# Block sums of a seven-product projection: added by DVE, or by accumulating transfers into the loaded block

## The chip, the cores and the metric

The kernel runs on one core of a Trainium2 chip. Its engines are TensorE (PE, with weight loads shown as PEld), VectorE (DVE), ScalarE (ACT), GpSimd (POOL) and SyncE (SP), and 16 DMA engines move data between the chip's main memory and the on-chip SBUF. The metric is the device time of one execution in microseconds. The weights are laid out by the host before the launch; that is not in the time.

## The reference, cut to what matters

Two groups of 512 tokens, each with 1024 features, pass through two layers with the same weights, and a last norm:

```python
for i in range(DEPTH):                       # 2: attention, then retention
    h = rms_norm(x, norm_g[i], NORM_EPS)
    ...
        x = x + diff_attention(h, da_w_in[j], ..., da_w_out[j], lambda_init)
    ...
        x = x + bidir_retention(h, ret_w_in[j], ..., ret_w_out[j])
return rms_norm(x, final_norm_g, NORM_EPS)
```

Both mixers begin with one wide projection, `proj = h @ w_in`, that yields queries, keys, values and a gate. It has 8192 columns in the first layer and 6144 in the second, and it is the projection that the change touches:

```python
proj = h @ w_in
q, k, v, gate = jnp.split(proj, [...], axis=-1)
```

After it, queries and keys are rotated by position, the mixer runs, its output is normed, multiplied by `silu(gate)` and multiplied by `w_out`.

## The kernel before

**Precision.** Every matmul operand is split in two float32r parts, high (`hi_of`, line 383, a cast on ACT) and low (`lo_of`, line 386, a subtraction on DVE), and a product is made of three matmuls: high by high, high by low, low by high (`PASSES`).

**Projection.** The two groups are multiplied by the same weights together. The 1024 input features are cut in two halves (index k) and the output columns of a unit in two halves (index i), so a unit is a product of 2 x 2 blocks for two token groups. It is computed with seven block products instead of eight, after Strassen and Winograd, named P1 to P7. On the side of the activations the sums of blocks are made once per layer (`make_b`). On the side of the weights each unit makes its own: `Unit.prep` at lines 525 to 558. P1, P2 and P4 take a loaded block. P5 takes x(1,0) + x(1,1), P6 takes that less x(0,0), P3 takes x(0,1) less that, P7 takes x(0,0) - x(1,0). These four sums are the calls of `combine` (line 529), DVE instructions of line 532 that write a buffer of the ring `st`. Then the block is split into a place of the ring `ws`, which has 7 places (`WS_BUFS`).

A unit is "pair" (256 columns; a block is 512 rows by 128 columns, 256 KB; a product is 12 matmuls of 512 tokens; one place of `ws`) or "wide" (512 columns of values; a block is 512 KB; a product is 48 matmuls of 256 columns; two places of `ws`). There are 24 pair and 4 wide units in the first layer, 16 and 4 in the second. The pair units are rotated queries and keys (`rot_done`) and gates (`gate_done`); the wide ones are values (`v_done`).

**Loads.** `take` (line 505) loads 512 rows by 256 columns, 512 KB, into one of 4 places of the ring `raw`, four pieces of 1 KB per partition. In a pair unit one load holds x(0,k) and x(1,k) side by side, and `half_view` or `parity_view` picks the columns of one half, which in the first layer are runs of 64 and in the second every other column. The same ring takes the output weights (`out_weights`, line 803) in the mixers' stages. The ring `st` has 3 places and also holds the decay tables of the retention layer (line 1137).

**After the product.** The seven products of a unit accumulate in PSUM banks named x, z and y (`BANK_OF`). ACT copies a bank (line 602) or DVE adds a bank to a copy (line 610); column half i = 0 is finished first, i = 1 later, and the `done` functions (lines 651 to 695) rotate, gate or split the finished half and store it.

**Order.** Nothing is issued directly. Every step is given to a planner (`Plan`) with its engine and an assumed cost, what it reads and what it writes. `Plan.arrange` runs a simulation: each engine takes, of the steps that are ready, the one with the earliest due time; PE may look 24 products ahead; loads are held until 15 us before they are due. Places of a ring are taken in turn. The order found is then issued, and each engine and each queue runs its own part strictly in that order. All transfers but four small ones are issued by SP; POOL makes only the small powers of the norms (lines 739, 740, 849, 851, 935, 936).

The stages are: norm and transposition of x, projections of layer one, attention with the output projection filled in between, projections of layer two, retention with its output projection, last norm.

Of the kernel before, what the change touches and what calls it, by code (L numbers as in the profile page):

```python
# [15 lines left out]
P = 128  # L16
S = 512
# [223 lines left out]
def trunk_kernel(  # L241
    ctx: ExitStack,
    tc: tile.TileContext,
    x_prompt, x_sample, norm_g, da_w_in, lq1, lk1, lq2, lk2, da_subln_g, da_w_out,
    ret_w_in, decay_fwd, decay_bwd, ret_subln_g, ret_w_out, final_norm_g,
# [136 lines left out]
    def hi_of(n, dst, src, r, w):  # L382
        act(n, lambda: nc.scalar.copy(dst(), src()), r, w)  # L383

    def lo_of(n, dst, src, hi, r, w):
        dve(n, lambda: nc.vector.tensor_tensor(dst(), src(), hi().bitcast(F32), op=ALU.subtract), r, w)  # L386
# [106 lines left out]
    class Unit:  # L493
        def __init__(self, w, c0, kind, done, view=None):


            self.w, self.c0, self.kind, self.done = w, c0, kind, done
            self.view = view or (lambda r, i: r[:, :, i * P:(i + 1) * P])
# [4 lines left out]
            self.banks = {}  # L503

        def take(self, i, k):

            if (i, k) not in self.x:
                c0 = self.c0 + (256 * i if self.wide else 0)
                r = slot(self.early + k, [P, 4, 256], F32) if self.early is not None else raw_t([P, 4, 256])
                src = self.w[k * S:(k + 1) * S, c0:c0 + 256].rearrange("(k p) c -> p k c", p=P)  # L510
                dma(lambda: r.t, lambda: src, [], [r], 512)
                if self.wide:
                    self.x[i, k] = ((lambda: r.t), r)
                else:
                    for n in range(2):
                        self.x[n, k] = ((lambda n=n: self.view(r.t, n)), r)
            return self.x[i, k]

        def like(self, t):

            if self.wide or len(self.x[0, 0][0]().shape) == 3:
                return t
            return t.rearrange("p k (j i) -> p k j i", j=2)

        def prep(self, op):
# [3 lines left out]
            def combine(a, b, fn):  # L529
                t = st_t([P, 4, n])  # L530
                out = ((lambda: self.like(t.t)), t)
                dve(4 * n, lambda: nc.vector.tensor_tensor(out[0](), a[0](), b[0](), op=fn), [a[1], b[1]], [t])
                return out
# [20 lines left out]
            hi_of(4 * n, lambda: self.like(hi[0]()), src[0], [src[1]], [hi[1]])  # L554
            lo_of(4 * n, lambda: self.like(lo[0]()), src[0], lambda: self.like(hi[0]()), [src[1], hi[1]], [lo[1]])
# [73 lines left out]
    def rot_done(dst, tab, scaled):  # L629
# [21 lines left out]
        def done(i, g, tiles, s, psum):  # L651
# [20 lines left out]
    def gate_done(dst, gc):  # L672

        def done(i, g, tiles, s, psum):
# [4 lines left out]
            dve(S, lambda: nc.vector.scalar_tensor_tensor(out.t, th.t, 1.0, x.t, op0=ALU.add, op1=ALU.mult),  # L679
# [6 lines left out]
    def v_done(dst):  # L686

        def done(i, g, tiles, s, psum):
            for u, x in enumerate(tiles):
                o = os_t()  # L690
                hi_of(S, lambda o=o: o[:, 0, :], lambda x=x: x.t, [x], [(o, 0)])
                lo_of(S, lambda o=o: o[:, 1, :], lambda x=x: x.t, lambda o=o: o[:, 0, :], [x, (o, 0)], [(o, 1)])
# [175 lines left out]
    w1, wo1, w2, wo2 = da_w_in[0], da_w_out[0], ret_w_in[0], ret_w_out[0]  # L868

    def half_view(r, i):  # L870
        return r.rearrange("p k (j two i) -> p k j two i", j=2, two=2)[:, :, :, i, :]

    def parity_view(r, i):
        return r.rearrange("p k (j i two) -> p k j i two", j=2, two=2)[:, :, :, :, i]
# [11 lines left out]
    def units1(tab):  # L886
        ropes = [Unit(w1, which * DI + h * 256, "pair",
                      rot_done({g: qk_d[0, which, h, g] for g in range(NG)}, tab, which == 0), half_view)
                 for h in range(NH) for which in range(2)]
        gates = [Unit(w1, 3 * DI + h * 256, "pair", gate_done({g: g_d[0, h, g] for g in range(NG)}, 16))  # L890
                 for h in range(NH)]
        wides = [Unit(w1, 2 * DI + h * 256, "wide",
# [4 lines left out]
    def units2(tab2):  # L897
        ropes = [Unit(w2, which * D + h * P, "pair",
                      rot_done({g: qk_d[1, which, h, g] for g in range(NG)}, tab2, which == 1), parity_view)
                 for h in range(0, NH, 2) for which in range(2)]  # L900
        gates = [Unit(w2, 2 * D + DI + h * 256, "pair", gate_done({g: g_d[1, h, g] for g in range(NG)}, 18))
                 for h in range(NH)]
        wides = [Unit(w2, 2 * D + h * 256, "wide",
# [339 lines left out]

def _tables():
# [40 lines left out]
```

## Time and profile before

| | us |
|---|---|
| median of 3 runs | 1864.89 |
| runs | 1857.8 to 1865.54 |
| span of the profiled execution, first to last instruction | 1856.5 |
| start, up to the steady projections | 72 |
| projections of layer one | 556 |
| hand-over and attention | 399 |
| hand-over to layer two | 50 |
| projections of layer two | 433 |
| retention, with its hand-over | 324 |
| last norm | 23 |

The stages are cut by eye from the trace's chain of waits. In the rows of the profile a line such as L386 is a line of the kernel; names left of the arrow are written, right of it are read, with buffer numbers left out; "b" and "arena" hold the activations' operands, "pj", "sc", "o" and "tp" are PSUM banks. A busy PE is not a PE at its peak, since the ends of matmuls are modelled; so the pace is read from the starts of products. Idle time before an instruction is followed by what released it.

### The profile page before, as it was taken

How to read it: one execution, taken by the hardware profiler on the slowest of the kernel's cores; microseconds unless marked ns; L12 is line 12 of the kernel's file. 1: busy time of each engine (PE TensorE's matmuls, PEld its weight loads, DVE VectorE, ACT ScalarE, POOL GpSimd, SP SyncE). 2: the span in 40 equal slices, each digit the busy share in tenths (PEclk: the TensorE clock that was granted, in tenths of full speed). 3: DMA queues.
4: the chain of work that ended last, by engine and by line, in shares of the span. 5: the costliest groups of instructions: out<-in, count | busy, mean ns of one | idle time of the engine just before them, and what ended most of it. 6: DMA issues, size and time to landing. Idle time of an engine off the chain costs nothing.

```text
span 1856.5 us, 27778 instructions
## 1 busy us (share of the span) xinstructions
PE 1823.4 (98%) x10337; PEld 1578.6 (85%) x10337; DVE 1450.6 (78%) x2423; ACT 926.7 (50%) x1897; POOL 152.8 (8%) x372
## 2 busy tenths in 40 slices
PE   6999999999999999999999999999999999999998
PEld 5888988988988878888888888989898988888886
DVE  7979688688688588888888896777777767766777
ACT  6734444343344465555555874435353454444444
POOL 3000000000000011111111300000000001111112
PEclk9999999999999999999999999999999999999999
DMA  4335544545545774444453433553545487434542
GB/s 161 119 119 182 182 136 153 177 124 181 160 126 173 266 272 179 182 170 153 153 183 125 159 97 103 168 170 130 174 143 165 142 313 268 169 146 168 195 145 91
DMA packets 149696, 307.31 MB, mean 166 GB/s; under 512 B 11940, under 2 KB 71992, under 8 KB 149560
## 3 DMA queue, kind: packets, MB, share of 16 engines
q1 hardware_dynamic: 149376, 305.45, 48.6%
q8 instruction: 81, 1.33, 0.3%
q14 instruction: 55, 0.45, 0.1%
q10 hardware_dynamic: 184, 0.08, 0.0%
HBM read 196.43 MB, written 109.05 MB: 165 GB/s over the span
## 4 chain that ended last, share of the span: by engine, by line
PE 91%; DVE 4%; ACT 2%; issue 1%; DMA 1%; POOL 1%; POOLq 0%; DVEq 0%; ACTq 0%
PE pj L573 22%; PE pj L824 18%; PE sc L573 11%; PE pj L580 9%; PE o L573 5%; PE o L1059 5%; PE o L1178 5%; PE sc L580 5%; PE sc L1007 5%; PE o L580 2%; PE sc L1160 2%; PE o L755 1%; PE tp L1043 1%; DVE ws L386 1%; DMA raw<-in_da_w_out_dram 1%
## 5 line engine op out<-in xcount | busy, mean ns | idle before, releaser
L824 PE MATMUL pj<-ws,arena 128*128 128x512 f32 x1536 | 399.5, 397 | 0.0
L824 PEld LDWEIGHTS pj<-ws,arena 128*128 128x128 f32 x1536 | 278.9, 188 | 54.1
L573 PE MATMUL pj<-b,ws 128*128 128x512 f32 x1200 | 293.6, 391 | 0.6 <-DVE e L610 0.6
L573 PEld LDWEIGHTS pj<-b,ws 128*128 128x128 f32 x1200 | 224.7, 188 | 49.6 <-issue 1.0
L829 DVE TENSOR_TENSOR b<-pj,b 128x512 f32<-128x512 f32 x256 | 176.1, 688 | 108.1 <-PE pj L824 107.7
L573 PE MATMUL sc<-arena,ws 128*128 128x512 f32 x960 | 232.3, 392 | 1.9 <-DVE arena L441 1.9
L386 DVE TENSOR_TENSOR ws<-st,ws 128x512 fp32r<-128x512 f32 (+1 forms) x192 | 148.1, 776 | 92.7 <-ACT ws L383 58.4
L573 PEld LDWEIGHTS sc<-arena,ws 128*128 128x128 f32 x960 | 180.1, 188 | 41.4 <-DVE arena L441 2.1
L386 DVE TENSOR_TENSOR ws<-raw,ws 128x512 fp32r<-128x512 f32 (+1 forms) x172 | 147.2, 861 | 83.5 <-ACT ws L383 72.4
L383 ACT CAST ws<-st 128x512 fp32r<-128x512 f32 (+1 forms) x192 | 131.9, 693 | 100.1 <-PE pj L573 35.8
L573 PE MATMUL pj<-arena,ws 128*128 128x512 f32 x720 | 177.5, 392 | 0.2 <-DVE arena L386 0.2
L383 ACT CAST ws<-raw 128x512 fp32r<-128x512 f32 (+1 forms) x172 | 130.8, 766 | 75.6 <-PE o L573 45.4
L739 POOL TENSOR_SCALAR css<-css 128x1 f32<-128x1 f32 x128 | 33.7, 263 | 1631.6 <-ACT o L737 918.3
L573 PEld LDWEIGHTS pj<-arena,ws 128*128 128x128 f32 x720 | 134.6, 188 | 29.3 <-DVE arena L386 0.5
L602 ACT COPY c<-pj 128x512 f32<-128x512 f32 x112 | 65.2, 583 | 128.5 <-PE pj L573 78.6
L573 PE MATMUL o<-arena,ws 128*128 128x512 f32 x480 | 116.0, 392 | 3.0 <-DVE e L441 3.0
L580 PE MATMUL pj<-ws,b 128*128 128x256 f32 x960 | 116.8, 276 | 0.0
L580 PEld LDWEIGHTS pj<-ws,b 128*128 128x128 f32 x960 | 113.2, 188 | 0.7
L1023 ACT ACTIVATE b<-sc,nm 128x512 f32<-128x512 f32 x128 | 88.0, 687 | 50.6 <-DVE nm L1015 50.5
L573 PEld LDWEIGHTS o<-arena,ws 128*128 128x128 f32 x480 | 89.4, 188 | 22.3 <-ACT ws L383 3.0
L1059 PE MATMUL o<-arena 128*128 128x256 f32 x768 | 106.8, 289 | 0.0
L1007 PE MATMUL sc<-arena 128*128 128x512 f32 x384 | 100.6, 398 | 4.0 <-ACT b L1023 4.0
(162 smaller groups left out, 2896.8 us busy)
## 6 DMA issues: line engine op xcount, KB each, us to landing
qk<-os SPq DMA_DIRECT2D x192, 256.0 KB, 3.9
arena<-qk SPq DMA_DIRECT2D x80, 512.0 KB, 4.8
raw<-in_da_w_in_dram SPq DMA_DIRECT2D x64, 512.0 KB, 5.1
v<-os SPq DMA_DIRECT2D x64, 512.0 KB, 4.2
arena<-v SPq DMA_DIRECT2D x64, 512.0 KB, 4.4
raw<-in_ret_w_in_dram SPq DMA_DIRECT2D x48, 512.0 KB, 4.2
os<-g SPq DMA_DIRECT2D x32, 512.0 KB, 7.5
g<-e SPq DMA_DIRECT2D x48, 256.0 KB, 4.4
```

Source lines behind the costliest of these rows:

```text
L383: act(n, lambda: nc.scalar.copy(dst(), src()), r, w)
L386: dve(n, lambda: nc.vector.tensor_tensor(dst(), src(), hi().bitcast(F32), op=ALU.subtract), r, w)
L573: nc.tensor.matmul(ps.t, a[u][0]()[:, k, :], bt[k][:, v, :], start=(opens and k == 0 and i == 0), stop=(k == 3 and i == 2), skip_group_che ...
L580: nc.tensor.matmul(ps[:, (t % 2) * 256:(t % 2) * 256 + 256], bt[k][:, v, t * P:(t + 1) * P], a[u][0]()[:, k, :], start=(opens and t % 2 == ...
L602: act(S, lambda c=c, ps=ps: nc.scalar.copy(c.t, ps.t), [ps], [c])
L824: nc.tensor.matmul(ps.t, o[a][:, e, t * P:(t + 1) * P], u[b][:, e, :], start=(n == 0), stop=(n == 5))
L829: dve(S, lambda: nc.vector.tensor_tensor(half, ps.t, half, op=ALU.add), [ps, (x, i)], [(x, i)])
L1007: nc.tensor.matmul(s.t, q[:, a, t * P:(t + 1) * P], k[:, b, :], start=(n == 0), stop=(n == 2))
L1023: act(840, lambda j=j, s=s, m=m: nc.scalar.activation(p[:, j, :], s.t, AF.Exp, bias=m.t, accum_out=sm[:, j:j + 1]), [s, m], [(p, j), (sm, j)])
L1059: nc.tensor.matmul(o[:, 0:256], aT[:, a, j * P:(j + 1) * P], v[b][:, j, :], start=(n == 0), stop=(n == 11))
L1160: nc.tensor.matmul(s.t, k[:, u, j * P:(j + 1) * P], q[:, v, :], start=(i == 0), stop=(i == 2))
L1178: nc.tensor.matmul(o[:, 0:256], a_[j][:, u, t * P:(t + 1) * P], v_[v][:, j, :], start=(n == 0), stop=(n == 11))
```

## The change

The host lays the weights of the input projections out in blocks: for each unit n, row half k and column half i, one block of 128 partitions by 4 times 128 (or 256) columns, contiguous in main memory, with the rotated pairs already sorted into halves. The kernel gets two such arrays per layer, `w1p` and `w1w`, `w2p` and `w2w`, in place of the plain weights.

`combine` is gone. A sum is now made by a transfer that adds a block from main memory into the block that lies in `raw`: `dma_add`, issued from POOL. P5, P6 and P3 are three successive states of one buffer, x(1,0): first x(1,1) is added, then x(0,0), then x(0,1). P7 is x(0,0) with x(1,0) added. As a transfer adds and does not subtract, column half i = 1 is computed with its sign turned: P4, P5 and P6 are negated when they are split, and the sign is taken back where half i = 1 is finished. `raw` gets 5 places, `st` keeps 2.

```diff
     def raw_t(shape):
-        return work("raw", shape, 4)
+        return work("raw", shape, 5)
     def st_t(shape, name="st"):
-        return work("st", shape, 3, name=name)
+        return work("st", shape, 2, name=name)
...
+    def dma_add(out, in_, w, kb):
+        plan.op("POOL", 1.1, lambda: nc.gpsimd.dma_start(out(), in_(), accum_op=ALU.add), [], w,
+                lands=2.5 + kb / 150.0, kb=2 * kb)
+
+    def hi_of(n, dst, src, r, w, sign=1):
+        if sign < 0:
+            act(n, lambda: nc.scalar.activation(dst(), src(), AF.Copy, scale=-1.0), r, w)
+        else:
+            act(n, lambda: nc.scalar.copy(dst(), src()), r, w)
+    def lo_of(n, dst, src, hi, r, w, sign=1):
+        if sign < 0:
+            dve(n, lambda: nc.vector.scalar_tensor_tensor(
+                dst(), src(), -1.0, hi().bitcast(F32), op0=ALU.mult, op1=ALU.subtract), r, w)
...
         def take(self, i, k):
             if (i, k) not in self.x:
                 if self.wide:
+                    r = raw_t([P, 1024])
+                    dma(lambda: r.t, lambda: self.block(i, k), [], [r], 512)
+                    self.x[i, k] = ((lambda: r.t), (r, None))
                 else:
+                    r = slot(self.early + k, [P, 2, S], F32) if self.early is not None else raw_t([P, 2, S])
                     for n in range(2):
+                        self.x[n, k] = ((lambda n=n: r[:, n]), (r, n))
+                    dma(lambda: r.t, lambda: self.w[self.n, k].rearrange("i p c -> p i c"), [], [r], 512)
...
-            def combine(a, b, fn):
-                t = st_t([P, 4, n])
-                out = ((lambda: self.like(t.t)), t)
-                dve(4 * n, lambda: nc.vector.tensor_tensor(out[0](), a[0](), b[0](), op=fn), [a[1], b[1]], [t])
-                return out
+            def add(to, i, k):
+                dma_add(to[0], lambda: self.block(i, k), [to[1]], 2 * n)
+                return to
+            sign = -1 if op in ("P5", "P6", "P4") else 1
...
             elif op == "P5":
-                src = self.s[1] = combine(x(1, 0), x(1, 1), ALU.add)
+                src = add(x(1, 0), 1, 1)
             elif op == "P6":
-                src = self.s[2] = combine(self.s[1], x(0, 0), ALU.subtract)
+                src = add(x(1, 0), 0, 0)
             elif op == "P3":
-                src = combine(x(0, 1), self.s[2], ALU.subtract)
+                src = add(x(1, 0), 0, 1)
             else:
-                src = combine(x(0, 0), x(1, 0), ALU.subtract)
+                src = add(x(0, 0), 1, 0)
...
-            hi_of(4 * n, lambda: self.like(hi[0]()), src[0], [src[1]], [hi[1]])
-            lo_of(4 * n, lambda: self.like(lo[0]()), src[0], lambda: self.like(hi[0]()), [src[1], hi[1]], [lo[1]])
+            hi_of(4 * n, lambda: flat(hi[0]()), src[0], [src[1]], [hi[1]], sign)
+            lo_of(4 * n, lambda: flat(lo[0]()), src[0], lambda: flat(hi[0]()), [src[1], hi[1]], [lo[1]], sign)
...
-            dve(S, lambda: nc.vector.tensor_tensor(m1.t, m1.t, m2.t, op=ALU.subtract), [m1, m2], [m1])
+            dve(S, lambda: nc.vector.tensor_tensor(m1.t, m1.t, m2.t, op=ALU.add), [m1, m2], [m1])
...
-            dve(S, lambda: nc.vector.tensor_tensor(a.t, a.t, m3.t, op=ALU.add), [a, m3], [a])
+            dve(S, lambda: nc.vector.tensor_tensor(a.t, a.t, m3.t, op=ALU.subtract), [a, m3], [a])
...
+            one = -1.0 if i else 1.0
...
+                sign = -1 if i else 1
```

The four waits that this makes: an accumulate waits until the block it adds into has landed or, for P6 and P3, until both parts of the operand before it have been read from that buffer; and the split behind it waits until the accumulate has landed.

More of the change, by code (lines that the diff above doesn't have):

```diff
@@ L493, in trunk_kernel, with __init__ @@
     class Unit:
[L494 to L498 removed]
+        def __init__(self, w, n, kind, done):
+            self.w, self.n, self.kind, self.done = w, n, kind, done
             self.wide = kind == "wide"
@@ L1241, with _blocks, cut @@
 _OUTS = [((1, S, D), 'float32'), ((1, S, D), 'float32')]
+def _blocks(w, ropes, halves, gates, wides):
+    import numpy as np
+    def cut(cols):
+        n = cols.shape[-1]
+        t = np.asarray(w)[0][:, cols.reshape(-1)].reshape(2, 4, P, len(cols), 2, n)
+        return np.ascontiguousarray(t.transpose(3, 0, 4, 2, 1, 5).reshape(len(cols), 2, 2, P, 4 * n))
+    step = np.arange(P)
+    side = np.arange(2)[:, None]
+    rope = step // 64 * P + (side * 64 + step % 64 if halves else step % 64 * 2 + side)
+    pair = [c0 + rope for c0 in ropes] + [c0 + side * P + step for c0 in gates]
+    wide = [c0 + side * 256 + np.arange(256) for c0 in wides]
+    return cut(np.stack(pair)), cut(np.stack(wide))
 def _tables():
@@ L1272 @@
     arrays, args = {}, []
-    named = [(n, _np.ascontiguousarray(_np.asarray(inputs[n]))) for n in _INS] + _tables()
+    named = []
+    for n in _INS:
+        if n == "da_w_in":
+            laid = _blocks(inputs[n], range(0, 2 * DI, 256), True, range(3 * DI, 4 * DI, 256), range(2 * DI, 3 * DI, S))
+        elif n == "ret_w_in":
+            laid = _blocks(inputs[n], range(0, 2 * D, 256), False, range(2 * D + DI, 2 * D + 2 * DI, 256),
+                           range(2 * D, 2 * D + DI, S))
+        else:
+            laid = [_np.ascontiguousarray(_np.asarray(inputs[n]))]
+        named += [(f"{n}{i}" if i else n, a) for i, a in enumerate(laid)]
+    named += _tables()
     for name, a in named:
```

52 lines of the change are left out of this document (20 added, 32 removed).

## The prediction

> **What bounds the kernel now.** I first read the page's busy totals and the chain that ended last.
>
> ```profile
> span 1856.5 us, 27778 instructions
> PE 1823.4 (98%) x10337; PEld 1578.6 (85%) x10337; DVE 1450.6 (78%) x2423; ACT 926.7 (50%) x1897; POOL 152.8 (8%) x372
> q1 hardware_dynamic: 149376, 305.45, 48.6%
> PE 91%; DVE 4%; ACT 2%; issue 1%; DMA 1%; POOL 1%; POOLq 0%; DVEq 0%; ACTq 0%
> ```
>
> PE is busy for 98% and makes 91% of the chain, DVE 4%. A busy PE need not be a PE at its peak, so the second view is the busy time by stage: start, first projections, hand-over to attention, hand-over to the second projections, those projections, end.
>
> ```profile
> core 0: us, PE busy (x) PEld busy (x) DVE busy (x) ACT busy (x) POOL busy (x), PEclk, DMA share, GB/s
> 0.00:72.00 72.00, 53.64 (x247) 43.81 (x248) 58.56 (x99) 46.32 (x79) 14.17 (x20) 1.00 0.38 129
> 72.00:628.00 556.00, 556.00 (x3108) 483.59 (x3107) 446.34 (x680) 244.78 (x409) 0.00 (x0) 1.00 0.51 159
> 628.00:656.00 28.00, 23.96 (x103) 19.45 (x102) 15.67 (x29) 13.67 (x27) 0.00 (x0) 0.89 0.80 314
> 1027.00:1077.00 50.00, 48.95 (x269) 40.49 (x266) 43.38 (x74) 41.55 (x91) 12.61 (x25) 1.00 0.45 151
> 1077.00:1510.00 433.00, 433.00 (x2571) 382.73 (x2570) 325.51 (x487) 202.29 (x331) 0.00 (x0) 1.00 0.47 150
> 1834.00:1857.00 23.00, 14.39 (x71) 11.68 (x69) 16.34 (x27) 8.91 (x27) 7.23 (x14) 0.88 0.36 138
> ```
>
> In both projections PE has no idle microsecond (556.00 of 556, 433.00 of 433), while DVE works 446.34 of 556, 80%. Whether PE also keeps its pace there is told by the chain in order of time, here around one two-head ("pair") unit:
>
> ```profile
> 132.22 2.75 PE sc L573 x12
> ...
> 151.45 2.75 PE sc L573 x12
> 154.19 2.75 PE pj L573 x12
> 156.94 2.75 PE sc L573 x12
> ```
>
> Each product of 12 matmuls takes 2.75 us and the next starts where it ends; from P5 of one unit (132.22) to P5 of the next (151.45) are 19.23 us, 7 products of 2.75 us. So nothing that DVE saves there can bring the end nearer. What can be won is where PE waits: 18.4 us at the start, 4.0 in the hand-over to attention, 8.6 at the end, which has no weight sums in it.
>
> **The change, part by part.**
>
> *The sums leave DVE.* One row of busy time by stage, for line 532 alone, has all of them:
>
> ```profile
> 0.00:1857.00 1857.00, 148.81 (x192) 1.00 0.49 165
> ```
>
> 192 instructions, 148.8 us of DVE. In the projections they lie beside a PE that never waits: worth 0 there. At the start DVE is what PE waits for:
>
> ```profile
> 33.80 8.50 PE L573 MATMUL o<-arena,ws 128*128 128x512 f32 x36 [2.76 <-DVE e L441]
> 45.92 5.78 PE L573 MATMUL sc<-arena,ws 128*128 128x512 f32 x24 [1.87 <-DVE arena L441]
> 71.54 3.69 PE L573 MATMUL pj<-b,ws 128*128 128x512 f32 x15 [0.62 <-DVE e L610]
> 40.95 0.68 DVE L532 TENSOR_TENSOR st<-st,raw 128x512 f32<-128x512 f32 x1
> 41.67 1.42 DVE L532 TENSOR_TENSOR st<-raw,st 128x512 f32<-128x512 f32 x2
> 50.73 0.69 DVE L532 TENSOR_TENSOR st<-raw 128x512 f32<-128x512 f32 x1
> 62.28 0.69 DVE L532 TENSOR_TENSOR st<-raw,raw 128x512 f32<-128x512 f32 x1
> 24.01 0.75 DVE L370 TENSOR_SCALAR b<-b,rsf 128x1024 f32<-128x1024 f32 x1
> 24.22 3.95 POOL L936 TENSOR_TENSOR rsf<-ssf,mhalf 128x1 f32<-128x1 f32 x1
> ```
>
> The 2.76 us before 33.80 hang on the second group's last norm on POOL (24.22 to 28.17), its scaling and transposes; the sums are not in that path: 0. Before 45.92 DVE runs without a gap, with three sums from 40.95 to 43.09; they take 2.1 us away from in front of line 441, so of the 1.87 us some 1.8 go. Before 71.54 stand two more sums, 1.4 us: the 0.62 goes. What is late next in either place is the product itself on PE. Sum of this part: **-2.4 us**.
>
> *The accumulating transfers.* A pair unit has four of 256 KB, a wide unit four of 512 KB, issued on POOL, whose queue holds nothing else in the projections. Three of the four form a chain in one buffer: P5's high and low part must be read before the next block is added for P6, and P6's before P3. In that chain ACT and DVE take part with
>
> ```profile
> L383 ACT CAST ws<-st 128x512 fp32r<-128x512 f32 x160 | 98.3, 621 | 72.7 <-PE pj L573 32.7 <-issue 16.0 <-PE sc L573 12.1
> L386 DVE TENSOR_TENSOR ws<-st,ws 128x512 fp32r<-128x512 f32 x160 | 109.1, 687 | 58.4 <-ACT ws L383 58.4
> L383 ACT CAST ws<-st 128x1024 fp32r<-128x1024 f32 x32 | 33.6, 1051 | 27.4 <-PE o L580 12.0 <-PE sc L573 8.6 <-PE pj L573 3.1
> L386 DVE TENSOR_TENSOR ws<-st,ws 128x1024 fp32r<-128x1024 f32 x32 | 39.0, 1220 | 34.2 <-PE sc L580 28.2 <-PE o L580 6.1
> 316.97 1.22 DVE L386 TENSOR_TENSOR ws<-st,ws 128x1024 fp32r<-128x1024 f32 x1
> 340.51 5.44 PE sc L580 x48
> ```
>
> How long may one accumulate take? The 7 places of `ws` let a pair unit's P5 be split as soon as P5 of the unit before has run, at 132.22 + 2.75 = 134.97. P3, the end of the chain, starts at 156.94. In these 21.97 us lie three splits of 0.62 + 0.69 = 1.31: 18.0 remain for two transfers, **9.0 us each**. For the wide unit the low part of P5 was done at 318.19 and P3 started at 340.51: 22.32 less two splits of 1.05 + 1.22 leaves 17.8, **8.9 us each**. Fetching into `raw` is no closer: 5 places for 4, at most 2 held by a pair unit.
>
> No row shows an accumulate. The nearest:
>
> ```profile
> raw<-in_da_w_in_dram SPq DMA_DIRECT2D x64, 512.0 KB, 5.1
> raw<-in_da_w_out_dram SPq DMA_DIRECT2D x16, 512.0 KB, 9.8
> cos<-in_rope_dram SPq DMA_DIRECT2D x1, 256.0 KB, 4.2
> ```
>
> From below 4.2 us (a plain 256 KB load), from above 9.8 (a 512 KB load in crowded stages). 256 KB more cost 0.9 between the first and the last row. An accumulate also has to fetch what it adds to, so I count its size twice, and add 1 us for POOL's part: 4.2 + 0.9 + 1 = 6.1 us for a pair, 5.1 + 2 x 0.9 + 1 = 7.9 for a wide unit. These are estimates. I take them, as the nearest rows are the loads of the same stage and not the crowded ones. Both are under their budgets, so PE waits **0 us**; the cover is the 2.9 and 1.0 us left. Behind a waiting accumulate on POOL stand only others; behind the waiting split on ACT stand the copies that free PSUM banks.
>
> *What else moves.* The engines' share of 51% rises: the loads before stay 512 KB in number and size, with longer rows, and 160 x 256 KB + 32 x 512 KB = 58.7 MB are added to 305.45 MB that made 48.6%: counted twice, +19% of the span, nearly all in the two projections (989 of 1856.5 us), where that is 35 points more, about 85%. That speaks for the upper half of the bounds. Where a weight is negated, ACT scales instead of casting and DVE uses a three-operand form:
>
> ```profile
> L679 DVE SCALAR_TENSOR_TENSOR e<-c,e 128x512 f32<-128x512 f32 x48 | 32.4, 686 | 2.8 <-ACT c L678 2.8
> L681 ACT ACTIVATE e<-e,gcol 128x512 f32<-128x512 f32 x48 | 34.4, 724 | 19.4 <-DVE e L679 19.3
> ```
>
> 686 for 687 ns on DVE, at most 724 for 621 on ACT, under a free half of ACT: 0. The swapped add and subtract, the negated constants: 0. `st` falls from 3 to 2 places, but only the decay tables are left in it, used one head at a time: 0; the loads of the next table are then held to a head ahead, 4 tiles of work: still early.
>
> *One rule against the change.* The POOL row above took 3.95 us, beginning while DVE scaled a row (24.01 to 24.76). The Trainium skill, "SBUF — State Buffer", section "Who interferes with whom", says that POOL writes a transfer's descriptors through ports it shares with DVE, and stands still while DVE holds them. The row agrees that POOL can be slow; no run so far shows it for a transfer. This is the mechanism of the first rival.
>
> **Sum.** 0 - 2.4 + 0 = -2.4 us on the profiled execution: 1856.5 to 1854.1. The runs shown have a median of 1864.89, 8.4 us above that span; the same difference gives **1862.5 us**.
>
> **The rivals.**
>
> *1, slower: the chain of accumulates is too long.* For it: the crowded load of 9.8 us, the rising share, and POOL's 3.95 us where the same row form is usually
>
> ```profile
> L740 POOL TENSOR_TENSOR crs<-css,mhalf 128x1 f32<-128x1 f32 x128 | 73.2, 571 | 10.6
> ```
>
> 0.57: 3.4 us longer. It decides from 9.0 us on. With 3.4 us more an accumulate takes 9.5 and 11.3: 0.5 us too long twice in each of 40 pair units and 2.4 twice in each of 8 wide ones, 40 + 38 = 78 us: 1862.5 + 78 = 1941. Anything between threshold and this gives 1863 to 1941. ACT waiting in order makes it worse. Against it: POOL has nothing else to do there, and DVE's work is mostly two-input subtractions. Chance 0.24, half of it under 1910.
>
> *2, faster: the hand-over to attention loses its stall.*
>
> ```profile
> 649.55 1.04 ACT L383 CAST ws<-raw 128x1024 fp32r<-128x1024 f32 x1 [2.85 <-DMA raw<-in_da_w_out_dram]
> 651.94 2.93 PE L1007 MATMUL sc<-arena 128*128 128x512 f32 x6 [4.04 <-ACT b L1023]
> ```
>
> ACT waits in order for an output weight's load, and the exponentials behind it are late; PE idles 4.04 us and runs the next six matmuls in 2.93 instead of about 1.4. With a fifth `raw` place and another order this may go: 4.0 + 1.5 = 5.5 us: 1862.5 - 5.5 = 1857.0. Against it: that load went out late on SP, and no sum was in its way. Chance 0.18.
>
> *3, a loss at both hand-overs into a projection.* POOL's norms of x gate PE (rsf at 24.22), and POOL now has accumulates in front of them in order. Two of them at 1 us, or one waiting 2 us for its load, in each of two places: +4 us: 1866.5, within the measurement's grain. Chance 0.12.
>
> *4, the change does not take work off the path but moves the bound to POOL's queue.* Four accumulates per pair unit of 19.23 us: from 4.8 us of POOL each on, POOL is the bound; at 6 us it is 4.8 us per unit, 40 units, +190: 2055. Against it: POOL's work is only to issue. Chance 0.04.
>
> **How the numbers follow.** Forecast (a PE as full as before) 0.42, rivals 0.24, 0.18, 0.12, 0.04. About 0.5%, 9.3 us, is what a measurement of this kernel can tell from no change. Faster by more (below 1855.6) needs rival 2 and 1.4 us besides, as from the 2.76 us at the start: half of rival 2, and 0.04 of the forecast's: 0.13. Slower by more: rivals 1 and 4 and a little of 3: 0.30. The rest, 0.57, within. Forecast's own range 1855 to 1868. The range from 1850 (rival 2 with the 2.76 us, 1854.2, and 4 us for the spread of the runs) to 1910 (half of rival 1) leaves out some 0.16 above and 0.04 below.
>
> **What would show it.** Right: line 532 gone; PE busy 100% in both projections with 2.75 us per product; the waits at 45.92 and 71.54 shorter; accumulates landing in 6 to 8 us; DVE in the first projections about 446 - 79 = 368 us. Wrong: gaps of PE before P6 or P3 that name an ACT copy or split, and splits that name an accumulate; landings over 9 us; POOL busy for most of the projections; a different stall at 650.

## The result, and the profile after

| | before | after |
|---|---|---|
| median of 4 runs, us | 1862.99 | 1887.75 |
| runs, us | 1857.8 to 1865.54 | 1882.68 to 1895.1 |
| span of the profiled execution, us | 1856.5 | 1884.6 |

The ratio of after to before is 1.0143 with a 95% interval of [1.0109, 1.0176]: slower, where the forecast was no change. The ratios here are taken over all runs, so they can differ a little from the quotient of the medians. The busy totals and the DMA queues of the page after (packets, MB, share of 16 engines' span):

```profile
span 1884.6 us, 28190 instructions
...
PE 1835.3 (97%) x10337; PEld 1582.8 (84%) x10337; DVE 1324.5 (70%) x2233; ACT 918.8 (49%) x1895; POOL 315.8 (17%) x564
...
q1 hardware_dynamic: 115584, 305.45, 46.9%
q0 software_dynamic: 27648, 58.73, 18.4%
```

DVE has lost 126 us of work (1450.6 to 1324.5), as the sums said. PE has the same 10337 matmuls and the span is 28.1 us longer. The busy time by stage, for the start, the first projections, the hand-over to attention and the second projections:

```profile
0.00:72.00 72.00, 56.59 (x261) 46.97 (x262) 57.22 (x96) 50.47 (x87) 22.74 (x33) 1.00 0.70 200
72.00:632.00 560.00, 548.26 (x3004) 472.75 (x3004) 370.63 (x563) 232.35 (x393) 85.00 (x97) 0.99 0.77 202
632.00:660.00 28.00, 27.00 (x158) 23.42 (x158) 12.33 (x22) 9.53 (x17) 1.73 (x2) 1.00 0.92 308
1084.00:1520.00 436.00, 431.15 (x2522) 378.22 (x2521) 274.23 (x413) 198.97 (x328) 62.02 (x71) 1.00 0.74 195
```

PE, which had no idle microsecond in either projection, is now idle for 11.7 us of the first 560 and 4.9 of the later 436. The start is better: 15.4 us idle where it was 18.4. PE's waits, first between 72 and 640 us, then between 1084 and 1560 (total, times, longest):

```profile
PE sc L585 <- ACT c L614: 7.6, 4, 3.2
PE pj L585 <- DVE e L622: 4.1, 3, 3.7
```

```profile
PE sc L585 <- ACT c L614: 3.1, 2, 2.3
PE pj L585 <- DVE e L622: 2.7, 2, 1.6
...
PE pj L585 <- ACT c L614: 1.4, 3, 0.5
```

The names matter. PE does not wait for a split weight (`ws`). It waits for lines 614 and 622, the copy on ACT and the sum on DVE that empty a PSUM bank. Those two were never changed. What holds them is told by the waits of all engines over the whole span:

```profile
ACT ws L389 <- DMA raw<-in_da_w_in_dram: 100.1, 25, 9.6
ACT ws L389 <- DMA raw<-in_ret_w_in_dram: 83.8, 19, 8.8
...
ACT ws L391 <- DMA raw<-in_da_w_in_dram: 33.3, 15, 3.6
...
ACT ws L391 <- DMA raw<-in_ret_w_in_dram: 24.2, 13, 5.5
```

ACT stands 241 us before splits (389 with the sign turned, 391 without) whose block has not landed. The timeline shows two such waits and their price:

```profile
144.56 0.63 ACT L389 ACTIVATE ws<-raw 128x512 fp32r<-128x512 f32 x1 [4.13 <-DMA raw<-in_da_w_in_dram]
...
146.33 0.86 POOL L384 DMA_DIRECT2D raw<-in_da_w_in_dram  x1 [9.49 <-DVE ws L395]
...
151.47 1.65 ACT L391 CAST ws<-raw 128x512 fp32r<-128x512 f32 x3
...
153.02 0.63 ACT L389 ACTIVATE ws<-raw 128x512 fp32r<-128x512 f32 x1
...
153.56 0.60 ACT L391 CAST ws<-raw 128x512 fp32r<-128x512 f32 x1
...
154.06 0.58 ACT L614 COPY c<-sc 128x512 f32<-128x512 f32 x1
...
154.69 3.04 PE L585 MATMUL sc<-arena,ws 128*128 128x512 f32 x12 [0.99 <-ACT c L614]
...
156.81 0.88 POOL L384 DMA_DIRECT2D raw<-in_da_w_in_dram  x1 [1.54 <-DVE ws L395]
...
157.57 2.91 PE L585 MATMUL pj<-b,ws 128*128 128x512 f32 x12
...
164.90 0.63 ACT L389 ACTIVATE ws<-raw 128x512 fp32r<-128x512 f32 x1 [9.26 <-DMA raw<-in_da_w_in_dram]
165.56 0.69 DVE L395 SCALAR_TENSOR_TENSOR ws<-raw,ws 128x512 fp32r<-128x512 f32 x1 [5.57 <-ACT ws L389]
166.17 0.68 DVE L622 TENSOR_TENSOR e<-pj,c 128x512 f32<-128x512 f32 x1
...
166.91 4.39 PE L585 MATMUL pj<-b,ws 128*128 128x512 f32 x12 [3.67 <-DVE e L622]
```

Two forms of one fault. At 151.47 five splits stand in a row. P6's split had waited until 144.56, so the accumulate for P3 went out only at 146.33 and P3's split was late; as the places of `ws` are taken in turn, the others came behind it. The copy of line 614 stands sixth, at 154.06, and PE waits 0.99 us. At 156.81 POOL issues an accumulate; its split starts at 164.90, 8.1 us later. DVE's half of that split stands ahead of the sum of line 622 in DVE's order, so the sum runs at 166.17, though its product had ended at 160.5 (157.57 + 2.91), and PE has idled 3.67 us. The 12 matmuls behind it then take 4.39 us instead of 2.91.

Were the accumulates slow? The DMA issues (count, KB, median us from issue to landing):

```profile
raw<-in_da_w_in_dram POOLq DMA_DIRECT2D x96, 256.0 KB, 6.2
...
raw<-in_ret_w_in_dram POOLq DMA_DIRECT2D x64, 256.0 KB, 6.0
...
raw<-in_da_w_in_dram POOLq DMA_DIRECT2D x16, 512.0 KB, 5.3
...
raw<-in_ret_w_in_dram POOLq DMA_DIRECT2D x16, 512.0 KB, 6.7
```

No: 6.0 to 6.2 us where 6.1 was estimated, and 5.3 to 6.7 where 7.9 was. These are medians. The accumulates alone took 3.6 us at the least, 6.0 in the middle and 9.8 at the most, and that longest one lies at the start. (Over plain loads and accumulates of `raw` together the longest is 15.7 us, a plain load at 13 us.) The planner, which wrote down the order, had counted 1.1 + 4.2 = 5.3 us for each pair accumulate.

Where PE's time went can be added up from the starts of its matmuls: what each takes to the next beyond its pace before (229 ns for 512 columns, 2.75 us / 12; 113.5 ns for 256 columns, the mean in its wide units). In us, by stretch of the span, with the kernels of the experiments below; the last column counts wide units that ran at 118 ns a matmul throughout, some 1.5 us each (336 matmuls by 4.5 ns), in the first and the second projections:

| kernel | 0–100 | 100–600 | 600–700 | 1100–1500 | 1500–1600 | units at 118 ns |
|---|---|---|---|---|---|---|
| before | 16.7 | 0.0 | 8.8 | 0.0 | 3.0 | 0, 0 |
| after | 13.0 | 18.6 | 8.2 | 8.9 | 7.0 | 1, 2 |
| e9_idle_adds | 17.5 | 3.6 | 10.9 | 0.4 | 6.2 | 1, 0 |
| e4_half | 12.6 | 0.1 | 6.8 | 0.0 | 3.4 | 0, 0 |
| e13_three | 13.6 | 10.5 | 8.4 | 5.4 | 3.2 | 3, 4 |
| e7_half_plus_zeros | 12.4 | 26.0 | 7.9 | 0.9 | 3.7 | 0, 0 |
| e5_short_chain | 13.0 | 5.6 | 9.1 | 5.6 | 4.2 | 0, 4 |
| e6_short_others | 12.9 | 11.0 | 8.6 | 1.5 | 6.4 | 2, 0 |
| e12_all_quarter | 13.0 | 4.8 | 9.2 | 0.0 | 3.9 | 4, 0 |

After against before: the start gives back 3.7 us, the projections take 18.6 + 8.9, of which three slow wide units make some 4.5, and the hand-over to retention takes 4.0. That is, to within 1 us, the 28 us of the two spans.

The waits are not spread over the units. In the projections all of PE's waits of more than 0.25 us lie in the two pair units ahead of a wide one. ACT's seven longest waits for a landing, 7.9 to 9.6 us, end at 164.9, 305.9, 442.5, 580.6, 1272.8, 1369.7 and 1467.3 us, each 17 to 20 us before the first product of a wide unit. In each of them the accumulate for P6 took 8.0 to 9.0 us from POOL's issue to the split, and SP had issued at least one of the wide unit's 512 KB loads within the 4 us before it. So the crowding by these loads is the likely reason for the late landings; no run moves these loads alone, so that much is not shown.

### The profile page after: what moved, and what is told of

The parts are those of the page before. It is cut to its first block, busy times and chain, and to the rows that moved or that the text cites. A ratio compares the mean times of both kernels' runs of the same rounds, so it can differ in the third digit from the quotient of the medians.

```text
span 1884.6 us, 28190 instructions
## 1 busy us (share of the span) xinstructions
PE 1835.3 (97%) x10337; PEld 1582.8 (84%) x10337; DVE 1324.5 (70%) x2233; ACT 918.8 (49%) x1895; POOL 315.8 (17%) x564
## 3 DMA queue, kind: packets, MB, share of 16 engines
q0 software_dynamic: 27648, 58.73, 18.4%
## 5 line engine op out<-in xcount | busy, mean ns | idle before, releaser
L585 PE MATMUL sc<-arena,ws 128*128 128x512 f32 x960 | 235.0, 395 | 13.1 <-ACT c L614 11.7
L398 DVE TENSOR_TENSOR ws<-raw,ws 128x512 fp32r<-128x512 f32 (+1 forms) x220 | 179.1, 841 | 88.3 <-ACT ws L391 81.0
L395 DVE SCALAR_TENSOR_TENSOR ws<-raw,ws 128x512 fp32r<-128x512 f32 (+1 forms) x144 | 111.6, 776 | 132.9 <-ACT ws L389 130.3
L389 ACT ACTIVATE ws<-raw 128x512 fp32r<-128x512 f32 (+1 forms) x144 | 100.7, 702 | 192.3 <-DMA raw<-in_da_w_in_dram 100.1
L391 ACT CAST ws<-raw 128x512 fp32r<-128x512 f32 (+1 forms) x220 | 156.0, 743 | 75.5 <-DMA raw<-in_da_w_in_dram 33.3
L384 POOL DMA_DIRECT2D raw<-in_da_w_in_dram x112 | 98.5, 949 | 523.9 <-DVE ws L395 271.8
L384 POOL DMA_DIRECT2D raw<-in_ret_w_in_dram x80 | 70.2, 922 | 384.9 <-DVE ws L395 164.9
```

Source lines behind the costliest of these rows:

```text
L384: plan.op("POOL", 1.1, lambda: nc.gpsimd.dma_start(out(), in_(), accum_op=ALU.add), [], w, lands=2.5 + kb / 150.0, kb=2 * kb)
L389: act(n, lambda: nc.scalar.activation(dst(), src(), AF.Copy, scale=-1.0), r, w)
L395: dve(n, lambda: nc.vector.scalar_tensor_tensor(dst(), src(), -1.0, hi().bitcast(F32), op0=ALU.mult, op1=ALU.subtract), r, w)
L585: nc.tensor.matmul(ps.t, a[u][0]()[:, k, :], bt[k][:, v, :], start=(opens and k == 0 and i == 0), stop=(k == 3 and i == 2), skip_group_che ...
```

## The experiments

In the expectations of e1 to e4, A is the theory that splits wait, in order, for landings later than the planner assumed and hold up the copies and sums behind them. In e5 to e7 it is narrowed to the chain P5, P6, P3, and in e9 to e11 A2 is the wider form again. B is the theory that the added traffic itself costs the time. Each ratio is to the kernel before, run on the same chip (its medians there were 1858.4 to 1859.4 us).

| kernel | median, us | ratio [95%] |
|---|---|---|
| e1_layout_alone | 1858.48 | 1.0006 [0.9991, 1.0021] |
| e2_layout_zero_adds | 1883.3 | 1.013 [1.0095, 1.0165] |
| e3_price_up | 1929.29 | 1.0393 [1.037, 1.0417] |
| e4_half | 1855.5 | 0.998 [0.9969, 0.9992] |
| e5_short_chain | 1864.96 | 1.0025 [1.0004, 1.0046] |
| e6_short_others | 1870.48 | 1.0056 [1.0036, 1.0076] |
| e7_half_plus_zeros | 1885.44 | 1.0137 [1.011, 1.0163] |
| e8_first_three | 1854.96 | 0.9975 [0.9958, 0.9992] |
| e9c_control | 1858.69 | 0.9997 [0.9982, 1.0012] |
| e9_idle_adds | 1868.37 | 1.0055 [1.0039, 1.0072] |
| e10_zeros_ahead | 1904.09 | 1.0238 [1.0203, 1.0272] |
| e11_ahead | 1893.52 | 1.0181 [1.0155, 1.0208] |
| e12_all_quarter | 1860.21 | 0.9991 [0.9973, 1.001] |
| e13_three | 1868.0 | 1.0034 [1.0017, 1.0051] |
| e14_pool_hi | 1960.93 | 1.0539 [1.0512, 1.0565] |

### The layout alone

The blocks of the change, but the sums by DVE as before, 4 places of `raw`, 3 of `st`, no sign turned:

```diff
-                src = add(x(1, 0), 1, 1)
+                src = self.s[1] = combine(x(1, 0), x(1, 1), ALU.add)
```

> Weights in blocks as in the change, but the four sums of a unit on DVE as before (raw 4 places, st 3, no signs turned, no accumulates). Theory A (in order: ACT and DVE stand behind an accumulate that lands later than the order assumed, and the PSUM copies and sums behind them release PE late): 1858 to 1866, as before. Theory B (traffic: the accumulates' 58.7 MB raise the DMA share to 77% and make everything late): the same, 1858 to 1866. Theory C (the layout itself, or where the buffers come to lie, costs: three of eight wide units ran at 118 ns a matmul for 113): 1868 or more, and wide units at 118 ns.

1.0006: the layout costs nothing and brings nothing. What is left of the change is the accumulates and what goes with them: the fifth place of `raw`, two places of `st`, the turned signs. e4 below has all of the latter and loses nothing, so the loss is due to the accumulates.

### Traffic that something waits for, and traffic that nothing waits for

e2 is e1 with an accumulate of 512 KB of zeros behind each load of a weight block, 60.8 MB:

```diff
                     dma(lambda: r.t, lambda: self.block(i, k), [], [r], 512)
+                    dma_add(lambda: r.t, lambda: zero_in, [r], 512)
```

> e1 and, behind each load of a weight block into raw, one accumulate of 512 KB of zeros onto it from POOL: 116 x 512 KB = 60.8 MB of accumulates, as much as in the change, but none between the products of a unit. Theory A: 1858 to 1870, no PE waits that name an ACT copy in the steady projections. Theory B: 1880 to 1895, as the change.

It lost as much as the change, but in part elsewhere. The waits of PE in e2:

```profile
PE o L956 <- DVE b L370: 9.1, 2, 8.0
...
PE o L956 <- ACT b L368: 6.4, 1, 6.4
PE sc L587 <- ACT c L616: 6.2, 2, 4.3
```

Line 956 transposes the normed x: POOL had accumulates in its queue ahead of the powers of the norms. That is rival 3 of the prediction, in a kernel that is not the change. Line 616 is the copy that empties a PSUM bank (line 614 of the change): in e2, too, splits wait for an accumulate, the one behind the load (ACT for 5.2 us before 1150.54, PE for 4.3 before 1155.63). So e2 does not tell A from B. e9c is e1 with 2 places of `st`; e9 is that with 212 accumulates of 256 KB into a buffer that nobody reads, each let out when the low part of one of the four sums has been made (a copy of one column on POOL waits for it). PE and SP run in the same order in both:

```diff
+            if late_on and op in ("P5", "P6", "P3", "P7"):
+                for c in range(2 if self.wide else 1):
+                    dummy(lo, lambda c=c: self.block(0, 0)[:, c * 512:c * 512 + 512])
```

> e1 (blocks, sums on DVE) with st 2 instead of 3 places: the control of e9, which needs that place. Both theories: 1855 to 1870; it counts only as what e9 is compared with.

> The control with accumulates of 256 KB of weights from POOL into a buffer that nothing reads, one per sum of a unit (two in a wide unit), each behind the split of its operand: some 200, 50 to 58 MB, with the order of the instructions on PE and SP unchanged and nothing waiting for them. Theory B (traffic itself): 20 us or more over the control, PE's waits in the projections as in the change. Theory A2 (an accumulate costs through what waits for its landing, and traffic only by making landings late): within 5 us of the control, with landings of loads and stores longer, and no PE waits in the steady projections.

e9 carries 55.6 MB, nearly the change's 58.7, and its engines are busier than the change's in the first projections (DMA share 0.83 against 0.77):

```profile
72.00:632.00 560.00, 558.50 (x3104) 484.44 (x3105) 450.69 (x682) 244.90 (x409) 171.56 (x237) 1.00 0.83 211
```

Its ratio is 1.0055, some 10 us, more than the 5 us that A2 allowed and half of what B asked for. By the table above 4.0 us of it lie in the projections (3.6 and 0.4, of which one slow wide unit makes 1.5), and some 6 at the start and the two hand-overs. The change loses 18.6 + 8.9 in its projections. So traffic for which nothing waits is a small part of that loss.

### How many of the four

e4 makes P5 and P7 by accumulates and P6 and P3 by DVE: 29.4 MB, no accumulate behind another.

```diff
-                src = add(x(1, 0), 0, 0)
+                src = self.s[2] = combine(self.s[1], x(0, 0), ALU.add)
...
-                src = add(x(1, 0), 0, 1)
+                src = combine(x(0, 1), self.s[2], ALU.add)
```

> The change with accumulates for P5 and P7 alone (both can run long before their split); P6 and P3 by DVE from st. Half the accumulate traffic, no chain of accumulates. Theory A: 1858 to 1867. Theory B: half of the loss, 1872 to 1880.

0.998: no loss, a small gain. Its accumulates, with half the traffic, are no faster than the change's, and ACT waits for them in order too; yet PE is full:

```profile
raw<-in_da_w_in_dram POOLq DMA_DIRECT2D x48, 256.0 KB, 5.9
...
raw<-in_ret_w_in_dram POOLq DMA_DIRECT2D x32, 256.0 KB, 6.3
```

```profile
72.00:632.00 560.00, 560.00 (x3125) 486.74 (x3124) 410.56 (x630) 244.61 (x408) 43.06 (x49) 1.00 0.67 186
```

An accumulate of 6 us is hidden where it stands alone. e13 adds P6, so that one accumulate stands behind another, 44.0 MB:

```diff
-                src = self.s[2] = combine(self.s[1], x(0, 0), ALU.add)
+                src = self.s[2] = add(x(1, 0), 0, 0)
```

> P5, P6 and P7 by accumulating transfers, P3 by DVE again into a buffer of st: 144 transfers, 44.0 MB, and a chain of one link (P5 to P6) in place of two. If the loss is a matter of bytes alone, it lies on the line between half of them (ratio 0.998 at 29.4 MB) and all (1.0143 at 58.7): about 1.006, 1870. If it is the chain, one link has the time of two (some 20 us from the split of P5 to the start of P3), nothing is late and it is like the half: 1855 to 1859.

1868.0 us lies between the two expectations, nearer the one by bytes (1870). In its profiled execution the loss of the second projections is four slow wide units and nothing else (5.4 us); in the first, 10.5 less three such units leaves some 6 to 7. e7 adds the other half's traffic to e4 as zeros behind each accumulate, so that the two stand in series ahead of P5's split and of P7's, and the chain to P6 and P3 is DVE's:

```diff
                 dma_add(to[0], lambda: self.block(i, k), [to[1]], 2 * n)
+                dma_add(to[0], lambda: zero_in[:, 0:4 * n], [to[1]], 2 * n)
```

> e4 (accumulates for P5 and P7 alone) with an accumulate of zeros of the same size behind each of them: 58.7 MB of accumulates as in the change, none between P5 and P3. Theory A: 1853 to 1866. Theory B, with a threshold above e4's traffic: 1880 to 1890.

1.0137, the change's loss without the change's chain: theory A, as it was narrowed to that chain, falls. The waits of e7:

```profile
PE sc L590 <- ACT c L619: 13.6, 3, 5.5
...
PE pj L590 <- DVE e L627: 5.3, 3, 3.8
```

The same two instructions are late (the numbers of the lines have moved), behind splits that wait for the zeros. What the change, e13 and e7 share, and e4 has not, is an accumulate behind another accumulate. But each of them also moves more bytes than e4 (58.7, 44.0 and 58.7 MB against 29.4), and no run puts two in series at e4's traffic. So these runs do not tell the second link from the crowding that it brings. Why nearly all of e7's loss is in the first layer stays open.

### Length with everything else kept

e5 and e6 keep the change's order and cut two of the four accumulates to a quarter of their columns; e12 cuts all four:

```diff
-                dma_add(to[0], lambda: self.block(i, k), [to[1]], 2 * n)
+                c = n if op in ('P6', 'P3') else 4 * n          # e5; e6: ('P5', 'P7'); e12: always n
+                dma_add(lambda: to[0]()[:, 0:c], lambda: self.block(i, k)[:, 0:c], [to[1]], 2 * n)
```

> The change in its own order, but the accumulates for P6 and P3 move only the first quarter of the columns (three quarters of these two sums are left out); those for P5 and P7 are whole. Theory A (P6's and P3's accumulates stand in series between products; what lands late holds ACT and DVE, and PE behind them): landing of the two falls by 1 us or more, and PE's lost time in the projections with it, 1858 to 1872. Theory B (traffic): 37% of the accumulate traffic is gone, so about as much of the loss as in e6, 1875 to 1882.

> As e5, the other way round: the accumulates for P5 and P7 move a quarter of their columns (three quarters of these two sums are left out), those for P6 and P3 are whole. The same bytes are gone as in e5, in the same order of instructions. Theory A: most of the loss stays, 1875 to 1888. Theory B: the same as e5.

> The change with each of its 192 accumulates cut to the first quarter of its columns (64 and 128 KB, 14.7 MB in all instead of 58.7), so three quarters of every sum are left out; the same waits, the same order of every engine, the same number of transfers on POOL. Theory C (PE waits because the landings are long and the splits wait for them in order): small ones landed in 3.4 to 3.6 us before, 2.6 us less than the whole ones, so the chain has 5.6 us of slack a link and no landing reaches the planner's assumed 4.2 us by much: PE's stalls in both projections go, only the gain at the start is left, 1853 to 1858. Theory D (the order of the splits and copies that the new waits make, whatever the landings take): the bursts of splits ahead of a PSUM copy stay, 1870 or more. Between the two, 1859 to 1869, means that both have a part.

With the same bytes in e5 and e6, shortening the chain's own two links leaves 1.0025, shortening the other two 1.0056: either cut takes most of the loss away, where A expected most of it to stay in e6 (1875 or more). The intervals touch, so no weight rests on the difference. e12 decides more. It has every wait, every order and every issue of the change; only the landings are shorter:

```profile
raw<-in_da_w_in_dram POOLq DMA_DIRECT2D x96, 64.0 KB, 3.9
raw<-in_ret_w_in_dram POOLq DMA_DIRECT2D x64, 64.0 KB, 3.9
```

and PE has no idle microsecond in the first projections:

```profile
72.00:632.00 560.00, 560.00 (x3099) 487.70 (x3098) 374.81 (x570) 236.93 (x398) 86.89 (x99) 1.00 0.59 168
```

At the place of the change's 3.67 us the same accumulate's split starts 5.1 us after POOL's issue instead of 8.1, and the sum behind it is in time:

```profile
152.74 0.88 POOL L384 DMA_DIRECT2D raw<-in_da_w_in_dram  x1 [1.96 <-DVE ws L395]
...
157.80 0.63 ACT L389 ACTIVATE ws<-raw 128x512 fp32r<-128x512 f32 x1 [3.93 <-DMA raw<-in_da_w_in_dram]
...
159.08 0.68 DVE L621 TENSOR_TENSOR e<-pj,c 128x512 f32<-128x512 f32 x1
...
161.28 2.91 PE L584 MATMUL pj<-b,ws 128*128 128x512 f32 x12
```

1860.21 us falls into the band that the expectation had for "both have a part", but the 4.8 us that PE loses in these projections are four wide units at 118 ns (the last reaches past 600 us); no stall is left. So the order alone costs nothing (D falls), and the stalls in the projections come with the landing time of accumulates for which splits wait. The traffic is cut along with it (a DMA share of 0.59 for 0.77), so e12 does not say how much of the landing time is size and how much crowding.

### Telling the planner, and loading earlier

e3 raises the planner's price of an accumulate by 3 us; e11 lets the loads out 25 us ahead instead of 15; e10 does the same to e7:

```diff
-                lands=2.5 + kb / 150.0, kb=2 * kb)
+                lands=5.5 + kb / 150.0, kb=2 * kb)      # e3
-    AHEAD = 15.0
+    AHEAD = 25.0                                        # e10, e11
```

> The change with the planner's assumed landing of an accumulate 3 us longer (5.5 + kb/150 in place of 2.5 + kb/150); only the order of instructions changes. Theory A: the splits stand later in ACT's order, behind the copies: PE's waits in the projections fall by more than half, 1865 to 1877. Theory B: no change beyond noise, 1882 to 1895.

> e7 (P5 and P7 by accumulate, zeros behind each, 58.7 MB) with loads let out up to 25 us before they are due in place of 15. Theory A2: load, sum and zeros have 10 us more before their split, the loss of e7 falls by half or more: 1855 to 1872. Theory B: as e7, 1880 to 1890.

> The change itself with loads let out 25 us before they are due. The chain P5, P6, P3 does not begin with a late load, so theory A2: little of the loss goes, 1875 to 1890. If late loads are the cause in the change too: 1860 to 1872. Theory B: 1880 to 1890.

All three missed. e3 and e10 are slower than the kernels they were made from; e11 cannot be told from the change (1.0181 and 1.0143, with intervals that overlap). In e3 PE's wait has another name:

```profile
PE sc L585 <- ACT ws L391: 36.4, 24, 2.7
```

Now it is the split itself that is late, 24 times. With 1.1 + 7.2 = 8.3 us a link the planner seems no longer to hide the chain, and to plan PE's waits. That would suit a budget smaller than the 9.0 us of the prediction, and it was not measured by itself. For e10 and e11 the order differs throughout, and why more time ahead does not help is open; in e11 PE's wait is mostly for line 622 (19.6 us in 17 times).

### ACT out of the wait

e14 makes the high part of the four sums on POOL, so ACT never waits for an accumulate:

```diff
-            hi_of(4 * n, lambda: flat(hi[0]()), src[0], [src[1]], [hi[1]], sign)
+            if op in ("P5", "P6", "P3", "P7"):
+                pool(4 * n, lambda: nc.gpsimd.tensor_scalar_mul(flat(hi[0]()), src[0](), float(sign)), [src[1]], [hi[1]])
+            else:
+                hi_of(4 * n, lambda: flat(hi[0]()), src[0], [src[1]], [hi[1]], sign)
```

> The change with the high part of P5, P6, P3 and P7 made by POOL in place of ACT, so ACT never waits for an accumulate; the bytes and the two links of the chain stay, DVE still waits for the low part. Theory C1 (ACT in order behind a late landing holds back the PSUM copies that PE needs): the waits of PE for ACT's copies go and the loss falls to the 5 to 10 us that the traffic alone cost, 1863 to 1870. Theory C2 (the landing is late for the product itself, or DVE's sums behind the low part are what PE needs): no better than the change, 1880 or more, with PE's waits naming DVE; POOL's slower copy lengthens each link by some 0.5 to 1 us and makes that worse.

```profile
L567 POOL TENSOR_SCALAR ws<-raw x192: 1477/1577/3446, 17.4 to 1611.2; 128x512 fp32r<-128x512 f32 x160, 128x1024 fp32r<-128x1024 f32 x32
```

POOL needs 1577 ns in the middle where ACT needs 0.63 us, and the next accumulate stands behind that on the same engine. The kernel became 100 us slower, PE waiting for POOL, DVE and ACT in turn. It lengthened the links more than was allowed for, so it does not tell C1 from C2; what is known of the standing in order is what the timeline of the change shows.

### A version that beats both

Of the whole change only the start gains. e8 is e4 with accumulates in the first three units of each layer only, 3.15 MB:

```diff
-                src = self.s[1] = add(x(1, 0), 1, 1)
+                src = self.s[1] = add(x(1, 0), 1, 1) if self.soon else combine(x(1, 0), x(1, 1), ALU.add)
```

> e4 with accumulates only in the first three units of each layer, DVE sums from st in all others. If e4's gain comes from the start, where PE waits for DVE: 1853 to 1857, as e4. If it comes from DVE's relief in the projections: 1858 to 1864, as before.

0.9975 [0.9958, 0.9992], like e4's 0.998 with nine times the bytes. The gain is at the start (12.1 us lost in the first 100 where before loses 16.7), where DVE is what PE waits for. It is faster than both kernels, by less than the 0.5% that the prediction called no change. e8 and e4 also have the fifth place of `raw`, which was not tried alone, so its part in the gain is not shown.

## Why the prediction was wrong

- **What bounds the kernel, and the sums' worth of 0 in the projections: right.** DVE fell to 370.63 us there (368 forecast) and nothing came of it.
- **-2.4 us at the start: near in size, in part by luck.** PE loses 3.7 us less in the first 100 us. But of the two waits that the prediction counted, only the 0.62 us before `pj` went; the 1.87 us before `sc` became 1.4, where 1.8 of it were to go. The rest of the gain is in two waits that it had counted at nothing: the 2.76 us before `o` became 1.75, and a wait of 1.03 us at 29.4 is gone. In e8 and e4 both counted waits are gone, and the 2.76 is still 2.92: there the term came out as it was argued.
- **The price of an accumulate: right in the middle for a pair unit, too high for a wide one.** 6.0 to 6.2 us for 6.1, 5.3 to 6.7 for 7.9. The share of the DMA engines came to 0.77 and 0.74 for "about 85%".
- **"Both are under their budgets, so PE waits 0 us": the step that failed.** Three things were wrong in it. It compared a typical landing with the budget, while just ahead of the wide units the accumulates for P6 took 8.0 to 9.0 us, nearly the whole budget of 9.0. It counted the chain at its bare instruction times: in a unit without a stall, the low part of P5 starts at 113.69 and its successor's accumulate at 114.79, that of P6 at 121.84 and 122.93, and P3's split comes at 129.40 for a product at 134.31, so 4.9 us were left. And it asked whether the chain's own product is late. None of PE's waits in the projections names a split. What is late are lines 614 and 622, which stand behind a waiting split on ACT and DVE. The prediction wrote that behind the split "stand the copies that free PSUM banks", and put no price on it. e12 shows that these stalls go with shorter landings at the same order, e9 that most of them go when nothing waits for the transfers, and e4 that single accumulates of the same length, with half the traffic, do not cause them.
- **Rival 1** has the right sign and the right place, and 1887.75 lies in its range of 1863 to 1941; its remark that ACT's waiting in order makes it worse names what the trace shows. Its threshold (9.0 us) and its cause (POOL slowed by DVE) are not what happened: the loss came with a median of 6.2 us and with 8.0 to 9.0 in the units that stalled. The rule of the Trainium skill ("SBUF — State Buffer", section "Who interferes with whom") did not show here; the same section infers that DVE's two-input form leaves descriptor writing alone, and that form is most of what DVE runs beside them. POOL's issues beside a DVE at 70% took, at the least, in the middle and at the most, in ns:

```profile
L384 POOL DMA_DIRECT2D raw<-in_da_w_in_dram x112: 859/872/1564, 12.7 to 639.7; - x112
```

- **Rival 2** did not happen: before attention PE still waits once for line 1031, 2.8 us where it was 4.0, and the stage's loss is 8.2 for 8.8. **Rival 3** was seen in e2 alone. **Rival 4** did not happen: POOL is busy for 17%.
- **Traffic.** The prediction gave the crowded engines no cost of their own. e9 has some 10 us of it, 4.0 in the projections and the rest at the start and the hand-overs. In the change only the hand-over to retention loses more than before (4.0 us), and 2.3 of that is again a wait for line 614, behind a split for which ACT had waited 5.5 us. How far the waits and the crowding add up in the projections was not separated.

## What to carry to other kernels

Where engines run their queues in order, price a new wait by what stands behind it on the waiting engine, with the late landings and not the middle one: here a transfer of 6 us in the middle, with a budget of 9, cost 1.4%, most of it ahead of the wide units, where it took 8 to 9. One such transfer ahead of a use was free, two in series, with more traffic, were not. And a saving on an engine is worth something only in the stage where the bound engine waits for it: accumulates in the first three units of each layer brought all there was to win.

## What was not expected of the hardware

- **An accumulate's length depends at least as much on where it stands as on its size.** In pair units, those for P6 and P3 took 3.4 to 3.6 us with 64 KB (e5) and 4.3 to 4.8 with 256 KB (e6); those for P5 and P7 took 5.6 to 5.8 with 64 KB (e6) and 6.4 to 6.9 with 256 KB (e5). So a cut one of the second kind is slower than a whole one of the first. Why was not tested.
- **Whole wide units run at 113 or at 118 ns a matmul**, with the granted clock near 1.00 in the windows around both. All eight of before, e1, e4 and e7 ran at 113 in their profiled executions; four of e12 and seven of e13 at 118. One unit costs some 1.5 us by it. What decides was not found, and it may be part of the spread of the runs, which was not tested.
- **A long stall costs PE its clock as well.** The busy time by stretch around the stall of 3.67 us in the change; the number after the five engines is the granted clock:

```profile
155.00:163.00 8.00, 8.00 (x36) 6.38 (x34) 3.48 (x6) 0.64 (x2) 1.16 (x2) 1.00 0.96 236
...
166.90:169.00 2.10, 2.09 (x5) 1.71 (x6) 2.07 (x4) 0.66 (x2) 1.57 (x2) 0.50 0.31 47
169.00:171.20 2.20, 2.20 (x9) 1.76 (x9) 2.20 (x4) 0.85 (x2) 0.00 (x0) 0.80 1.03 192
171.20:174.00 2.80, 2.80 (x14) 2.31 (x13) 1.41 (x3) 0.86 (x3) 0.00 (x0) 1.00 1.05 278
```

  It fell to 0.50 and was back some 3 to 4 us later. So the 12 matmuls took 4.39 us instead of 2.91, and the stall cost 1.5 us more than its length; after the idle 0.99 us before 154.69 they took 3.04. The Trainium skill, "TensorE: Matmul & The Clock Gate", section "Part 1: The HAM clock gate", has the clock halved after an idle window of some 3.4 us; the row agrees with it. Over the runs the length of the wait does not decide by itself: a wait of 2.04 us in e13 (at 299.8) halved the clock, and one of 3.22 us in e7 (at 276.6) did not.
